# Attention's probability-value products as one 129-column matmul, with both heads of a tile in one PSUM bank

## The chip, the cores and the metric

The kernel runs on one core of one Trainium2 chip. The metric is device time in microseconds (us) of one execution of the whole program, as a median over runs. A profile of one further execution gives the durations of single instructions, the idle time of each engine and what ended it.

## What is computed

The reference is a two-layer encoder trunk on 2048 tokens of width 1024. Each layer normalises its input, projects it to 4096 columns, runs two kinds of heads side by side, gates both with a silu and projects back:

```
proj = rms_norm(x, gain) @ w_in            # aq ak av ag | rq rk rv rg
# A: 8 heads x 64, softmax over the own chunk of 64 and 8 chunks before it, with a relative bias
scores = q @ k.T * 64**-0.5 + bias ;  p = softmax(scores) ;  ya = p @ v
# B: 4 heads x 128, chunkwise retention with a state carried from chunk to chunk, and a norm per head
x = x + concat[ya * silu(ag), yr * silu(rg)] @ w_out
```

The change is in the last step of A: the product of the probabilities with the values, the division by the sum of the probabilities, and the gate.

## The kernel before

**Number format.** Products that need more than fp16 are split: a value is stored as an upper fp16 half and a lower fp16 half, and a product is the sum of three products of halves (upper-upper, upper-lower, lower-upper). The value tile `v` holds for each 128-token tile and head 129 columns: 64 upper halves, a column of ones, 64 lower halves. The column of ones makes the matmul deliver the sum of the probabilities as a 65th output column.

**Tiling.** For a layer `l`, `s` counts four slices of the heads (two attention heads and one retention head each), and `n` counts four blocks of 512 tokens. For each `(l, s, n)` there are the dense projections `dense_T` (L654, q and k and the retention's q and k, transposed) and `dense_V` (L785, values and gates), and later the `attention` (L823) of the same block, which runs beside the dense projections of the next block. A block has four tiles `a` of 128 tokens and two heads `hx`, so eight units. A unit looks back over `nb` of up to five 128-token blocks; there are 256 units and 1120 blocks in all.

**Order.** The order on TensorE, ScalarE, VectorE and GpSimd is written out by hand. `run` (L1219) takes the dense projections in rounds of eight 512-column matmuls. After each round it calls `tick`, which emits what is due on the deferred list (`later(k, fn)` puts `fn` k ticks ahead), and then one step of the attention. A unit takes three rounds. At its first round comes `flow`, which emits `pv` (L860) for the unit two before, and then `qk` (L830) for the new unit: the scores `S` on TensorE (L845, L846), bias and maximum on VectorE (L849, L851), the exponential and its upper half on ScalarE (L852, L854), the lower half on GpSimd (L855), and the transposing DMA `pT` (L857). The retention of a tile (L909) adds two groups of products `r1` and `r2` per six rounds, with VectorE and ScalarE work between them (L918, L903, L907: mask, upper half and rest of `dT`; L939: the state). Weight preparation for later slices is pushed into the same rounds; each weight section needs a sum over partitions, a one-column matmul `allsum` (L334).

**PSUM.** `psR` is a ring of four banks under the tag "small". In order of allocation it is used by `o` (the output of `pv`), `r1`, `r2` and the one-column sums. A new tile in a bank waits until the last reader of the tile before it is done. `psD` holds two banks for the dense projections; L697, L680 and L815 are the VectorE instructions that read them last.

**Around the change.** `pv` runs, for each block, three matmuls into 65 columns of a bank of its own (L865 to L867): upper probabilities with upper values and ones, upper probabilities with lower values, lower probabilities with upper values and ones. One tick later VectorE takes the reciprocal of the sum (L871), multiplies it by a constant (L872) and applies it and the gate (L877). After the second head of a tile the 128 columns are stored to DRAM by a DMA on SyncE's queue (L880).

Of the kernel before, what the change touches and what calls it, by code (L numbers as in the profile page):

```python
# [10 lines left out]
F32 = mybir.dt.float32  # L11
I32 = mybir.dt.int32
AF = mybir.ActivationFunctionType
ALU = mybir.AluOpType
# [4 lines left out]
P = 128  # L19
# [8 lines left out]
def hybrid_trunk(ctx: ExitStack, tc: tile.TileContext, x, pos, gain, gcol, w_in, w_out, rel, fgain,  # L28
# [8 lines left out]
    act, dve, pool, pe, sp = nc.scalar, nc.vector, nc.gpsimd, nc.tensor, nc.sync  # L37
# [5 lines left out]
    b2 = ctx.enter_context(tc.tile_pool(name="b2", bufs=2))  # L43
# [7 lines left out]
    psR = ctx.enter_context(tc.tile_pool(name="psR", bufs=4, space=PSUM))  # L51
# [16 lines left out]
    y_d = [dp.tile([P, D], F32, tag=f"y_d{t}", name=f"y_d{t}") for t in range(NT)]  # L68
# [554 lines left out]
    def in_turn(i):  # L623

        if not ring.get("free"):
            return
        tc.keep_in_program_order(i)


    def flow(k=0):  # L630

        if len(pipe) > k:
            pipe.pop(0)()
# [3 lines left out]
    def later(k, fn):  # L637
        deferred.append([k, fn])
# [184 lines left out]
    def attention(l, s, n, g, st, prev):  # L823
        units = []
        for a in range(4):
            for hx in range(2):
                units.append((a, hx))
        ya = {}

        def qk(a, hx):  # L830

            u = St()
            u.a, u.hx = a, hx
            u.nm = f"{l}_{s}_{n}_{a}_{hx}"
            u.nb = nb = min(5, 4 * n + a + 1)
            u.w = w = nb * P
            u.kts = [(st if t // 4 == n else prev, t % 4) for t in range(4 * n + a + 1 - nb, 4 * n + a + 1)]
            S = psS.tile([P, 1024], F32, tag="S", name=f"S{u.nm}")
            cs = slice(a * P, (a + 1) * P)
            cuts = sorted({0, nb} | {j for j in range(nb) if u.kts[j] == (st, 0) or j == 4})  # L840
            for j0, j1 in zip(cuts, cuts[1:]):
                q_, a_ = u.kts[j0]
                k_ = q_.k[:, hx, a_ * P:(a_ + j1 - j0) * P]
                o = S[:, j0 * P:j1 * P]
                pe.matmul(o, st.q[:, hx, 0, cs], k_, start=True, stop=False)  # L845
                pe.matmul(o, st.q[:, hx, 1, cs], k_, start=False, stop=True)  # L846
            v = b2.tile([P, 640], F32, tag="sc", name=f"sc{u.nm}")[:, 0:w]
            m = b2.tile([P, 1], F32, tag="mq", name=f"mq{u.nm}")
            dve.tensor_tensor_reduce(out=v, in0=S[:, 0:w], in1=g.bias[hx][:, 640 - w:640], scale=1.0, scalar=-3.0e38,  # L849
                                     op0=ALU.add, op1=ALU.max, accum_out=m)  # L850
            dve.tensor_scalar(m, m, g.nc[:, 0:1], LN_PSC, op0=ALU.mult, op1=ALU.add)  # L851
            act.activation(v, v, AF.Exp, bias=m[:, 0:1], scale=g.c[:, 0:1])  # L852
            pq = b2.tile([P, 1280], F16, tag="pq", name=f"pq{u.nm}")
            act.activation(pq[:, 0:w], v, AF.Copy)  # L854
            pool.tensor_tensor(pq[:, w:2 * w], v, pq[:, 0:w], op=ALU.subtract)  # L855
            u.p = b2.tile([P, 10, P], F16, tag="pT", name=f"pT{u.nm}")[:, 0:2 * nb, :]
            later(1, lambda: sp.dma_start_transpose(out=u.p, in_=pq[:, 0:2 * w]))  # L857
            return u

        def pv(u):  # L860
            t = 4 * n + u.a
            o = psR.tile([P, 512], F32, tag="small", name=f"o{u.nm}")
            for b, (q_, a_) in enumerate(u.kts):
                v_ = q_.v[:, a_, u.hx, :]
                pe.matmul(o[:, 0:65], u.p[:, b, :], v_[:, 0:65], start=(b == 0), stop=False)  # L865
                pe.matmul(o[:, 0:64], u.p[:, b, :], v_[:, 65:129], start=False, stop=False)  # L866
                pe.matmul(o[:, 0:65], u.p[:, u.nb + b, :], v_[:, 0:65], start=False, stop=(b == u.nb - 1))  # L867

            def out_():
                rl = b2.tile([P, 1], F32, tag="rl", name=f"rl{u.nm}")  # L870
                dve.reciprocal(rl, o[:, 64:65])  # L871
                dve.tensor_tensor(rl, rl, g.ka, op=ALU.mult)  # L872
                if u.hx == 0:
                    ya[u.a] = b2.tile([P, P], F32, tag="ya", name=f"ya{u.nm}")
                y = ya[u.a]
                vs = slice(u.hx * 64, u.hx * 64 + 64)
                dve.scalar_tensor_tensor(out=y[:, vs], in0=o[:, 0:64], scalar=rl[:, 0:1], in1=st.g[u.a][:, vs],  # L877
                                         op0=ALU.mult, op1=ALU.mult)
                if u.hx == 1:
                    later(1, lambda: in_turn(sp.dma_start(y_d[t][:, s * P:(s + 1) * P], y)))  # L880

            later(1, out_)

        ret = retention(l, s, n, g, st)
        rounds_ret = (5, 10, 10, 14, 14, 18, 18, 23) if (l, s, n) == (0, 0, 0) else [6 * a + b for a in range(4) for b in (0, 5)]
        for i, (a, hx) in enumerate(units):
            flow(1)
            u = qk(a, hx)
            for r in range(3 * i, 3 * i + 3):
                for _ in range(rounds_ret.count(r)):  # L890
                    next(ret, None)
                if r % 3 == 2:
                    pipe.append(lambda u=u: pv(u))
                yield
# [319 lines left out]
    def grp(l, s):  # L1214
        if (l, s) not in groups:
            groups[l, s] = Grp()
        return groups[l, s]
# [138 lines left out]
    for j in range(4):  # L1356
        o = VSEC[j] * 512
# [80 lines left out]
    for l in range(DEPTH):  # L1438
        gO = [Grp(), Grp()]
        go = Grp()  # L1440
        for s in range(NSW):
            g = grp(l, s)
            for n in range(NS):
                first = (l, s, n) == (0, 0, 0)
                if not first:
                    st = St()
                    states[l, s, n] = st
                    dT = dense_T(l, s, n, g, st)
                else:
                    st = st0  # L1450
# [129 lines left out]
```

## Time and profile before

| | |
|---|---|
| median of 3 runs | 2058.18 us (2057.85 to 2062.8) |
| span of the profiled execution | 2060.7 us |
| TensorE busy | 1999.4 us (97%), 14038 matmuls |
| VectorE busy | 1228.1 us (60%) |
| ScalarE busy | 1134.8 us (55%) |
| GpSimd busy | 688.1 us (33%) |
| mean granted TensorE clock | 0.995 |

The profiled execution's own time is its span of 2060.7 us, 2.5 us above the median of the runs. In the rows below, PE is TensorE's matmul side, PEld its weight loads, DVE VectorE, ACT ScalarE, POOL GpSimd and SP SyncE. [...] A group's row gives its busy time, the mean duration of one instruction in ns, and the engine's idle time just before it with what ended that.

### The profile page before, as it was taken

The page shows a single profiled execution, that of the slowest core. Times are in us where ns is not written, and L with a number is a line of the kernel's source. Part 1 is how long each engine was busy: PE and PEld are TensorE (multiplying, and loading weights), DVE is VectorE, ACT ScalarE, POOL GpSimd, SP SyncE. Part 2 cuts the span into 40 slices and gives each one's busy share as a digit, 9 for nine tenths or more (in the row PEclk, how much of TensorE's full clock was granted, in tenths as well). Part 3 has the DMA queues.
Part 4 walks back from the last instruction along what each step waited for, and adds up shares of the span by engine and source line. Part 5 has one row for each costly group of instructions (what it writes and reads, how often), then busy time and mean ns, then how long its engine had stood idle before and what let it go on. Part 6 is the DMA issues. An engine that isn't in the chain of part 4 may idle for free. (4 is left out here: it accounts for less than half of the span.)

```text
span 2060.7 us, 39339 instructions
## 1 busy us (share of the span) xinstructions
PE 1999.4 (97%) x14038; PEld 1052.9 (51%) x14038; DVE 1228.1 (60%) x3804; ACT 1134.8 (55%) x2526; POOL 688.1 (33%) x701
## 2 busy tenths in 40 slices
PE   6988999999999999999999999999999999999998
PEld 4444555555555555554444555555555555555544
DVE  6776666565556555666553556555655566557643
ACT  6556665556565645555444546655656565455432
POOL 0344343434334434430003443444333334333100
PEclk9999999999999999999999999999999999999999
DMA  8778664547584754899774546554746775658864
GB/s 227 169 161 178 155 148 109 112 114 164 117 185 113 165 128 101 174 209 263 219 185 113 124 104 156 116 126 103 158 117 150 148 155 124 129 115 187 224 203 139
DMA packets 645701, 313.64 MB, mean 152 GB/s; under 512 B 459232, under 2 KB 602080, under 8 KB 645504
## 3 DMA queue, kind: packets, MB, share of 16 engines
q1 hardware_dynamic: 645504, 311.12, 65.6%
q8 instruction: 110, 1.80, 0.4%
q14 instruction: 87, 0.71, 0.1%
HBM read 123.26 MB, written 41.98 MB: 80 GB/s over the span
## 5 line engine op out<-in xcount | busy, mean ns | idle before, releaser
L855 POOL TENSOR_TENSOR pq<-sc,pq 128x640 f16<-128x640 f32 (+4 forms) x256 | 319.4, 1248 | 860.5 <-ACT pq L854 443.8
L852 ACT ACTIVATE sc<-sc,mq,cT 128x640 f32<-128x640 f32 (+4 forms) x256 | 218.4, 853 | 615.6 <-DVE rl L871 309.7
L797 PE MATMUL dV<-whV,hTh 128*128 128x512 f16 x1024 | 353.9, 381 | 7.3 <-DVE gt L815 6.1
L797 PE MATMUL dV<-whV,hTl 128*128 128x512 f16 x1024 | 353.8, 381 | 0.0
L797 PE MATMUL dV<-wlV,hTh 128*128 128x512 f16 x1024 | 353.8, 381 | 0.0
L778 PE MATMUL dT<-hTh,whT 128*128 128x512 f16 x1008 | 346.6, 379 | 2.7 <-DVE kk L697 1.3
L778 PE MATMUL dT<-hTl,whT 128*128 128x512 f16 x1008 | 346.6, 379 | 0.0
L778 PE MATMUL dT<-hTh,wlT 128*128 128x512 f16 x1008 | 346.6, 379 | 0.0
L797 PEld LDWEIGHTS <-hTh 128*128 128x128 f16 x2048 | 197.0, 98 | 224.7 <-DVE gt L815 10.0
L778 PEld LDWEIGHTS <-whT 128*128 128x128 f16 x2016 | 192.1, 98 | 207.7 <-issue 1.6
L849 DVE CUSTOM_DVE_ANT_0 sc<-S,bias 128x640 f32<-128x640 f32 (+4 forms) x256 | 188.3, 735 | 88.8 <-PE S L846 87.4
L1172 PE MATMUL dO<-whO,yly 128*128 128x512 f16 x504 | 191.0, 379 | 1.7 <-DMA yly<-hTl 1.1
L1172 PE MATMUL dO<-whO,yhy 128*128 128x512 f16 x504 | 191.0, 379 | 1.0 <-DMA yhy<-hTh 1.0
L1172 PE MATMUL dO<-wlO,yhy 128*128 128x512 f16 x504 | 191.0, 379 | 0.0
L854 ACT ACTIVATE pq<-sc 128x640 f16<-128x640 f32 (+4 forms) x256 | 171.5, 670 | 8.1
L797 PEld LDWEIGHTS <-hTl 128*128 128x128 f16 x1024 | 99.4, 98 | 112.4 <-issue 3.9
L1172 PEld LDWEIGHTS <-yhy 128*128 128x128 f16 x1008 | 98.1, 98 | 113.7 <-DMA yhy<-hTh 1.5
L778 PEld LDWEIGHTS <-wlT 128*128 128x128 f16 x1008 | 97.2, 98 | 113.7 <-issue 6.0
L845 PE MATMUL S<-k,q 128*128 128x128 f16 (+3 forms) x592 | 142.4, 267 | 0.0
L865 PE MATMUL o<-v,pT 128*128 128x65 f16 x1120 | 129.8, 193 | 6.4 <-DMA pT<-pq 5.5
L866 PE MATMUL o<-v,pT 128*128 128x64 f16 x1120 | 130.1, 195 | 0.0
L846 PE MATMUL S<-k,q 128*128 128x128 f16 (+3 forms) x592 | 129.7, 267 | 0.0
(359 smaller groups left out, 3476.5 us busy)
## 6 DMA issues: line engine op xcount, KB each, us to landing
q<-qq SPq DMA_DIRECT2D x128, 128.0 KB, 2.4
yyy<-y_d SPq DMA_DIRECT2D x32, 512.0 KB, 4.5
stT<-in_w_in_dram SPq DMA_DIRECT2D x27, 512.0 KB, 4.8
stV<-in_w_in_dram SPq DMA_DIRECT2D x26, 512.0 KB, 4.6
k<-kk SPq DMA_DIRECT2D x128, 64.0 KB, 2.0
swp<-rot SPq DMA_DIRECT2D x64, 128.0 KB, 3.1
tabc<-tab SPq DMA_DIRECT2D x32, 256.0 KB, 3.0
tabs<-tab SPq DMA_DIRECT2D x32, 256.0 KB, 3.1
```

What stands on the lines that cost most here:

```text
L778: pe.matmul(ps, w_[:, j, kt, :], h_[:, kt, :], start=(m == 0), stop=(m == 23))
L797: pe.matmul(ps, h_[:, kt, a * P:(a + 1) * P], w_[:, kt, :], start=(m == 0), stop=(m == 23))
L845: pe.matmul(o, st.q[:, hx, 0, cs], k_, start=True, stop=False)
L846: pe.matmul(o, st.q[:, hx, 1, cs], k_, start=False, stop=True)
L849: dve.tensor_tensor_reduce(out=v, in0=S[:, 0:w], in1=g.bias[hx][:, 640 - w:640], scale=1.0, scalar=-3.0e38, op0=ALU.add, op1=ALU.max, accu ...
L852: act.activation(v, v, AF.Exp, bias=m[:, 0:1], scale=g.c[:, 0:1])
L854: act.activation(pq[:, 0:w], v, AF.Copy)
L855: pool.tensor_tensor(pq[:, w:2 * w], v, pq[:, 0:w], op=ALU.subtract)
L865: pe.matmul(o[:, 0:65], u.p[:, b, :], v_[:, 0:65], start=(b == 0), stop=False)
L866: pe.matmul(o[:, 0:64], u.p[:, b, :], v_[:, 65:129], start=False, stop=False)
L1172: pe.matmul(ps, h_[:, kt, :], w_[:, kt, :], start=(m == 0), stop=(m == 23))
```

## The change

The upper probabilities are multiplied with all 129 columns of `v` in one matmul, so that upper and lower values come out in separate columns of PSUM; the lower probabilities follow with 65 columns as before. Both heads of a tile write into one bank, 256 columns apart. Nothing is read after the first head. One tick after the second head's matmuls, ScalarE copies the lower values' products of both heads to SBUF and VectorE takes both reciprocals. One tick later VectorE adds the copy to the upper part (into free columns of the same bank), scales, and applies the gate for both heads in one instruction each. The DMA to DRAM moves by one tick with it. The tile `ya` now belongs to this step, and the ring `psR` is allocated from three times in six rounds and not four.

```diff
         def pv(u):
             t = 4 * n + u.a
-            o = psR.tile([P, 512], F32, tag="small", name=f"o{u.nm}")
+            if u.hx == 0:
+                ya[u.a] = psR.tile([P, 2, 256], F32, tag="small", name=f"o{u.nm}")
+            o = ya[u.a]
             for b, (q_, a_) in enumerate(u.kts):
                 v_ = q_.v[:, a_, u.hx, :]
-                pe.matmul(o[:, 0:65], u.p[:, b, :], v_[:, 0:65], start=(b == 0), stop=False)
-                pe.matmul(o[:, 0:64], u.p[:, b, :], v_[:, 65:129], start=False, stop=False)
-                pe.matmul(o[:, 0:65], u.p[:, u.nb + b, :], v_[:, 0:65], start=False, stop=(b == u.nb - 1))
+                pe.matmul(o[:, u.hx, 0:129], u.p[:, b, :], v_, start=(b == 0), stop=False)
+                pe.matmul(o[:, u.hx, 0:65], u.p[:, u.nb + b, :], v_[:, 0:65], start=False, stop=(b == u.nb - 1))
+            if u.hx == 0:
+                return
+            y = b2.tile([P, 2, 64], F32, tag="ya", name=f"ya{u.nm}")
+            rl = b2.tile([P, 2, 1], F32, tag="rl", name=f"rl{u.nm}")
+
+            def halves():
+                act.activation(y, o[:, :, 65:129], AF.Copy)
+                dve.reciprocal(rl, o[:, :, 64:65])
 
             def out_():
-                rl = b2.tile([P, 1], F32, tag="rl", name=f"rl{u.nm}")
-                dve.reciprocal(rl, o[:, 64:65])
-                dve.tensor_tensor(rl, rl, g.ka, op=ALU.mult)
-                if u.hx == 0:
-                    ya[u.a] = b2.tile([P, P], F32, tag="ya", name=f"ya{u.nm}")
-                y = ya[u.a]
-                vs = slice(u.hx * 64, u.hx * 64 + 64)
-                dve.scalar_tensor_tensor(out=y[:, vs], in0=o[:, 0:64], scalar=rl[:, 0:1], in1=st.g[u.a][:, vs],
-                                         op0=ALU.mult, op1=ALU.mult)
-                if u.hx == 1:
-                    later(1, lambda: in_turn(sp.dma_start(y_d[t][:, s * P:(s + 1) * P], y)))
-
-            later(1, out_)
+                w = o[:, :, 192:256]
+                dve.tensor_tensor(w, y, o[:, :, 0:64], op=ALU.add)
+                dve.scalar_tensor_tensor(out=w, in0=w, scalar=g.ka[:, 0:1], in1=rl.to_broadcast([P, 2, 64]), op0=ALU.mult,
+                                         op1=ALU.mult)
+                dve.tensor_tensor(y, w, st.g[u.a][:, 0:P].rearrange("p (h d) -> p h d", h=2), op=ALU.mult)
+                yf = y.rearrange("p h d -> p (h d)")
+                later(1, lambda: in_turn(sp.dma_start(y_d[t][:, s * P:(s + 1) * P], yf)))
+
+            later(1, halves)
+            later(2, out_)
```

## The prediction

> **What bounds the kernel now.** I read the page's first part, then the table of stretches. Columns of a stretch: its length, then the busy time of PE, PEld, DVE, ACT and POOL.
>
> ```profile
> span 2060.7 us, 39339 instructions
> PE 1999.4 (97%) x14038; PEld 1052.9 (51%) x14038; DVE 1228.1 (60%) x3804; ACT 1134.8 (55%) x2526; POOL 688.1 (33%) x701
> ```
>
> ```profile
> 80.00:360.00 280.00, 261.50 (x1839) 136.35 (x1838) 179.99 (x588) 170.47 (x384) 104.78 (x106) 0.98 0.68 148
> 1100.00:1360.00 260.00, 260.00 (x1875) 137.75 (x1874) 147.37 (x521) 147.53 (x351) 98.53 (x98) 1.00 0.53 120
> ```
>
> TensorE is the bound: in the middle of layer 1 it is busy for all of 260 us, and only in the first attention blocks does it lose something (18.5 of 280 us). A TensorE saving counts in full, and a new wait costs only if TensorE ends up waiting. So I next read who waits for whom (total us, times, longest).
>
> ```profile
> DVE sc L849 <- PE S L846: 87.4, 89, 2.4
> ACT sc L852 <- DVE rl L871: 309.7, 106, 3.9
> ACT sc L852 <- DVE mq L851: 250.9, 124, 3.5
> PEld L899 <- DVE dT L907: 12.8, 11, 2.6
> PEld L797 <- DVE gt L815: 10.0, 5, 3.8
> ```
>
> ```profile
> PE r L899 <- DVE dT L907: 6.8, 9, 1.6
> PE dV L797 <- DVE gt L815: 6.1, 4, 3.3
> PE msV L334 <- DVE ya L877: 3.4, 3, 1.5
> ```
>
> These rows carry the forecast. Of 256 score scans (L849) VectorE waits for TensorE before 89 only; at the other 167 the scores lay ready and VectorE came late. ScalarE's exponential waits on VectorE in 106 + 124 = 230 of 256 units. So VectorE runs behind TensorE in most units, although it is busy 60% of the time: its loss is in the order of its queue. Its lateness reaches TensorE in 11 + 5 + 9 + 4 + 3 = 32 places, 39.1 us together, 1.2 us each.
>
> **Part 1: the matmuls.** The timeline of TensorE over one unit (start, duration):
>
> ```profile
> 1204.74 0.19 PE L865 MATMUL o<-v,pT 128*128 128x65 f16 x1
> ...
> 1205.18 0.19 PE L867 MATMUL o<-v,pT 128*128 128x65 f16 x1
> 1205.21 0.38 PE L845 MATMUL S<-k,q 128*128 128x512 f16 x1
> ...
> 1205.75 0.33 PE L899 MATMUL r<-rot,rot 128*128 128x128 f16 x3
> 1205.92 0.38 PE L778 MATMUL dT<-hTh,wlT 128*128 128x512 f16 x1
> ```
>
> ```profile
> L865 PE MATMUL o<-v,pT 128*128 128x65 f16 x1120 | 129.8, 193 | 6.4 <-DMA pT<-pq 5.5 <-DVE ya L877 0.8
> L866 PEld LDWEIGHTS <-pT 128*128 128x128 f16 x1120 | 104.9, 97 | 28.6 <-issue 0.6
> ```
>
> The 15 products of a unit start within 1204.74 to 1205.21, 0.47 us: 31 ns each, 94 ns for the three of a block. Three 128-column products take 0.17 us (1205.75 to 1205.92): 57 ns each, and 129 columns the same. After the change a block costs 57 + 31 = 88 ns, so 6 ns less, times 1120 blocks: **7 us saved**. Bounds: 0 if the short product behind a long one costs 37 ns, 11 us if they cost 55 and 29. The columns that pass through the array stay the same (65 + 64 + 65 against 129 + 65 per block); only the spacing of one short product goes.
>
> The removed products' weight loads take 97 ns each, but follow each other at 31 ns beside the products, so nothing more comes from them. [...]
>
> **Part 2: the new wait.** VectorE and ScalarE around a second head's output now:
>
> ```profile
> 1212.30 0.82 DVE L849 CUSTOM_DVE_ANT_0 sc<-S,bias 128x640 f32<-128x640 f32 x1 [0.42 <-PE S L846]
> ...
> 1213.30 0.16 DVE L871 RECIPROCAL rl<-o 128x1 f32<-128x1 f32 x1
> 1213.49 0.16 DVE L872 TENSOR_TENSOR rl<-rl,kaV 128x1 f32<-128x1 f32 x1
> 1213.69 0.28 DVE L877 SCALAR_TENSOR_TENSOR ya<-o,rl,gt 128x64 f32<-128x64 f32 x1
> 1216.38 0.69 DVE L697 SCALAR_TENSOR_TENSOR kk<-dT,kk 128x512 f16<-128x512 f32 x1 [2.41 <-ACT kk L694]
> 1216.99 0.28 DVE L939 SCALAR_TENSOR_TENSOR state<-r,state 128x128 f32<-128x128 f32 x1
> 1219.00 0.83 DVE L849 CUSTOM_DVE_ANT_0 sc<-S,bias 128x640 f32<-128x640 f32 x1 [1.72 <-PE S L846]
> ```
>
> ```profile
> 1213.48 0.92 ACT L852 ACTIVATE sc<-sc,mq,cT 128x640 f32<-128x640 f32 x1 [3.14 <-DVE rl L871]
> 1214.43 0.74 ACT L854 ACTIVATE pq<-sc 128x640 f16<-128x640 f32 x1
> ...
> 1215.76 0.60 ACT L694 ACTIVATE kk<-dT 128x512 f16<-128x512 f32 x1 [0.39 <-PE dT L778]
> ```
>
> In the changed program's built order the reciprocal of every one of the 128 tiles waits for ScalarE's copy of the lower half, not for TensorE; the copy stands behind the exponential and the copy of the unit just started:
>
> ```
> VectorE: L849, L851 | Reciprocal rl<-o 128x2 [waits Activation] | L880 | L881 | L883 | L697 or L811 to L815 | state | L849
> ScalarE: L852 exp, L854 copy | L875 ya<-o 128x128 | evacuation of the dense product
> ```
>
> [...]
>
> Prices of the new steps from the nearest shapes:
>
> ```profile
> L903 ACT ACTIVATE dT<-r 128x128 f16<-128x128 f32 x128 | 33.5, 261 | 0.4 <-DVE r L918 0.4
> L918 DVE TENSOR_TENSOR r<-r,msk 128x128 f32<-128x128 f32 x128 | 37.1, 290 | 0.0
> L956 DVE SCALAR_TENSOR_TENSOR yr<-r,rss,gt 128x128 f32<-128x128 f32 x128 | 44.4, 347 | 23.5 <-POOL rss L952 22.5
> L805 ACT ACTIVATE v<-dV 128x128 f16<-128x128 f32 x128 | 33.5, 261 | 11.8 <-PE dV L797 11.4
> L806 ACT ACTIVATE gt<-dV,ughV 128x256 f32<-128x256 f32 x128 | 59.2, 462 | 0.5 <-DVE ya L877 0.4
> L807 ACT ACTIVATE rv<-dV,urvV 128x128 f16<-128x128 f32 x128 | 46.5, 363 | 0.0
> ```
>
> ScalarE's copy: 0.26 us. VectorE: 0.16 + 0.29 + 0.35 + 0.29 = 1.09 us and three hand-overs of 0.03 us (1213.30 + 0.16 to 1213.49): 1.2 us, where two heads now take about 2 x 0.67 us (1213.30 to 1213.97). So work falls slightly; the waiting is what counts. In this tile the reciprocal would wait from 1213.30 until the copy behind L854 is out at 1215.4, and the chain ends at 1216.6, not 1213.97: 2.6 us later.
>
> Behind it in VectorE's queue are the rest of the dense product (L697, or L811 to L815), the state, the next score scan, and `dT`'s rest (L907); ScalarE's next exponential waits for that scan, TensorE for L907 and, through psD, for L697 and L815. Much of the 2.6 us is covered, as L697 waits for ScalarE today (2.41 us). What cover remains is ScalarE's evacuation after the copy. In a `dense_T` round that is 0.60 us, so L697 comes later by 0.26 + (1.2 - 0.6) = 0.86 us; in a `dense_V` round it is 0.26 + 0.46 + 0.36 = 1.08 us, so 0.26 + (1.2 - 1.08) = 0.38 us. Mean **d = 0.62 us** per tile; lower end 0.2 us (this tile, where ScalarE had 0.39 us to spare: 1216.6 against 1216.38), upper end the whole 2.6 us where nothing behind waits for ScalarE.
>
> Where VectorE waits for the scores (1.72 us before the last scan above), d costs nothing. Where TensorE already waits for VectorE, it costs d in full: 32 x 0.62 = 20 us. Near misses come on top: 32 waits spread over a mean of 1.2 us suggest 32 x 0.62 / 1.2 = 17 places within reach, at half of d: 5 us. **25 us lost**; with the lower end 6 + 1 = 7 us, and with 0.86 us in every tile 28 + 10 = 38 us.
>
> **Part 3: the ring.** With three tiles per six rounds in a ring of four banks, a bank comes round after eight rounds, not six, and `o` is held from the first head's product until the gate of both. Its own products are late enough for that, but the one-column sums fall in between. There are 55 of them:
>
> ```profile
> L334 PEld LDWEIGHTS <-ones x55: 97/98/105, 0.9 to 1685.3; 128*128 128x128 bf16 x55
> ```
>
> In the built order 11 wait for L883, where 9 wait for L877 now, of which 3 cost 3.4 us. With the bank free 2.6 us later I let all 11 wait those 1.1 us: 12 - 3.4, about **8 us lost**; bounds 0 and 11 x 2.6 = 28 us.
>
> **Moved at no cost.** The store's DMA is issued one tick later, in SyncE's order in front of the next unit's transposes; the transposes of the unit under way stand before it. If that cover goes, `pT` comes late: TensorE's wait for it at L865 is 5.5 us in all today.
>
> **Sum.** 2060.7 - 7 + 25 + 8 = 2086.7 us as a span; the median of the runs lies 2.5 us below the span: **2084 us**, slower by 1.3%. A measurement of this kernel can tell about 0.3% (6 us) from no change.
>
> **Rivals.**
> - *The waits stay hidden, TensorE's saving is left.* The place is the middle of the layers, where TensorE has no idle time and VectorE's wait for ScalarE is there anyhow. For it: 1100 to 1360 us. Against it: 167 late scans. 2058 - 7 = 2051 us. It decides if VectorE's chain still ends before L697 and L815 could start. Chance 0.15.
> - *Both about cancel:* d at its lower end and no ring waits, -7 + 7: 2058 us. Chance 0.10.
> - *VectorE and ScalarE become the bound.* If the 2.6 us fall on VectorE uncovered in the 32 places and the 17 become 32 x 2.6 / 1.2 = 69 at half, that is 83 + 90 us less what the queue catches up; already half of it gives 2058 + 87 - 7 + 8 = 2146 us. Against it: VectorE is free 40% of the time. Chance 0.09.
> - *Weight loads are paid in full.* If each removed load costs its 97 ns, 1120 x 97 = 109 us go: 1949 us. Against it stands the 31 ns spacing. Chance 0.02. [...]
>
> **The numbers.** The forecast as worked out has 0.64. Its own bounds are 2058 - 11 + 7 = 2054 and 2058 + 38 + 28 - 7 = 2117 us. The range of 2050 to 2118 takes in the second rival and the centre of the first; left out are the third, the fourth and some of the first, about 0.18. Slower by over 0.3%: 0.64 + 0.09 = 0.73; within 0.3%: 0.10; faster: 0.15 + 0.02 = 0.17.
>
> **What would show it.** TensorE's unit of ten products should take 5 x 88 = 0.44 us for 0.47, PE's busy time fall by some 7 us and its idle time rise by 30 to 40 us. The waits should name VectorE's reciprocal waiting for ScalarE's L875, about 2 us in most of the 128 tiles, and TensorE waiting longer for `dT` (L913) and, at L334, for L883. I am wrong if TensorE's waits for VectorE stay near 39 us in total: then the cover held. If they grow, but at the accesses of `pT` or `S`, the place was wrong.

## The result, and the profile after

The changed kernel takes 2088.6 us (median of 4 runs, 2087.37 to 2089.82) against 2059.3 us of the kernel before beside it: a ratio of 1.0137, 95% interval 1.0123 to 1.0152, so 28 us slower by the ratio and 29 us by the two medians. The forecast was 2084 us.

The page of the kernel after, first part:

```profile
span 2085.6 us, 37004 instructions
PE 2005.0 (96%) x12918; PEld 1049.8 (50%) x12918; DVE 1205.8 (58%) x3548; ACT 1155.2 (55%) x2654; POOL 680.6 (33%) x701
```

There are 1120 matmuls fewer, and yet TensorE is busy for 5.6 us longer (1999.4 before) and idle for 80.6 us instead of 61.3. Its unit of ten products, on the timeline of the kernel after (start, duration):

```profile
1230.67 0.22 PE L867 MATMUL o<-v,pT 128*128 128x129 f16 x1
1230.73 0.20 PE L868 MATMUL o<-v,pT 128*128 128x65 f16 x1
...
1231.08 0.19 PE L868 MATMUL o<-v,pT 128*128 128x65 f16 x1
1231.11 0.38 PE L845 MATMUL S<-k,q 128*128 128x512 f16 x1
```

From 1230.67 to 1231.11 it is 0.44 us for the ten, where the fifteen took 0.47. Each is shown with 0.19 to 0.22 us and starts 0.03 to 0.06 us ahead of the next, so the unit is counted from start to start and not by the shown durations. So the matmuls did what the diff says; the loss is elsewhere. The waits of the kernel after (total us, times, longest):

```profile
DVE rl L876 <- ACT ya L875: 250.8, 120, 4.7
DVE sc L849 <- PE S L846: 40.4, 50, 2.0
ACT sc L852 <- DVE mq L851: 558.2, 232, 5.1
PEld L905 <- DVE dT L913: 30.8, 30, 3.5
```

and those of TensorE's two sides alone:

```profile
PE r L905 <- DVE dT L913: 24.0, 25, 3.7
PE msV L334 <- DVE ya L883: 4.8, 3, 2.6
PE msT L334 <- DVE mbT L327: 4.8, 5, 1.7
PE msO L334 <- DVE ya L883: 2.1, 2, 1.1
PE dV L797 <- DVE gt L815: 3.9, 5, 1.6
PEld L334 <- DVE ya L883: 8.7, 6, 2.8
PEld L797 <- DVE gt L815: 6.7, 8, 2.1
```

The first row is the new wait: the reciprocal stands for 250.8 us in 120 of the 128 tiles behind ScalarE's copy, 2.1 us each. The second shows how far VectorE fell behind: it came to the score scan before TensorE had the scores 89 times before the change and 50 times now. The price is paid where TensorE waits for `dT`.

The rows of PEld and of PE must not be added up, though the prediction adds them: they show the same stalls from two sides. One stall of the kernel after, on the timelines of the two sides (start, duration, idle time before it):

```profile
195.04 0.10 PEld L905 LDWEIGHTS <-dT 128*128 128x128 f16 x1 [1.27 <-DVE dT L913]
195.05 0.23 PE L905 MATMUL r<-rv,dT 128*128 128x128 f16 x1 [1.10 <-DVE dT L913]
```

In the kernel before, all 9 waits of PE for `dT` and all 4 for `gt` lie within a wait of PEld; in the kernel after it is 24 of 25 for `dT`, and 5 of 5 each for `gt` at L797 and for `ya` at L334. PE's side is the idle time of the matmuls: 24.0 us for `dT`, where it was 6.8; at the one-column sums (L334) 4.8 + 2.1 = 6.9 us for 3.4; at the dense values (L797) it fell, 3.9 for 6.1. Together that is 34.8 us in place of 16.3, a rise of 18.5 us, near the 19.3 us by which TensorE's idle time rose in all. A wait that the kernel before does not have, 4.8 us in 5 places for `mbT` (L327, VectorE's weight preparation), comes up as well, and other waits fell. The prediction and the expectations count both sides together; on that scale `dT` is 30.8 + 24.0 = 54.8 us in place of 19.6.

VectorE around one tile's gate, on the timeline of the kernel after:

```profile
1232.73 0.21 DVE L851 TENSOR_SCALAR mq<-mq,ncT 128x1 f32<-128x1 f32 x1
1235.12 0.17 DVE L876 RECIPROCAL rl<-o 128x2 f32<-128x2 f32 x1 [2.18 <-ACT ya L875]
1235.32 0.30 DVE L880 TENSOR_TENSOR o<-ya,o 128x128 f32<-128x128 f32 x1
1235.65 0.36 DVE L881 SCALAR_TENSOR_TENSOR o<-o,kaV,rl 128x128 f32<-128x128 f32 x1
1236.05 0.29 DVE L883 TENSOR_TENSOR ya<-o,gt 128x128 f32<-128x128 f32 x1
1236.26 0.68 DVE L697 SCALAR_TENSOR_TENSOR kk<-dT,kk 128x512 f16<-128x512 f32 x1
1238.53 0.82 DVE L849 CUSTOM_DVE_ANT_0 sc<-S,bias 128x640 f32<-128x640 f32 x1 [1.39 <-PE S L846]
```

VectorE has nothing to do for 2.18 us, although reciprocal, gate and L697 are queued. The four instructions of the gate end at 1236.34, 1.22 us after the reciprocal's start. Here the scan behind them still has 1.39 us to wait, so at the scan this tile costs nothing; one without that slack passes its lateness on.

The stretches of the kernel after (columns as in the prediction; behind POOL's the granted clock, the DMA share and GB/s):

```profile
80.00:360.00 280.00, 254.08 (x1615) 131.27 (x1614) 170.30 (x518) 166.28 (x386) 101.54 (x104) 0.96 0.66 144
1100.00:1360.00 260.00, 258.46 (x1673) 134.78 (x1672) 135.59 (x439) 143.20 (x352) 96.67 (x101) 1.00 0.54 122
```

Between 80 and 360 us TensorE is idle 25.9 us for 18.5 before, 7.4 of the 19.3 us, and its clock is 0.96 for 0.98. In the middle of layer 1, where it had no idle time, it now has 1.5 of 260 us.

### The profile page after: what moved, and what is told of

Its sections match the earlier page's. It is cut to its first block, busy times and chain, and to the rows that moved or that the text cites. A ratio compares the mean times of both kernels' runs of the same rounds, so it can differ in the third digit from the quotient of the medians.

```text
span 2085.6 us, 37004 instructions
## 1 busy us (share of the span) xinstructions
PE 2005.0 (96%) x12918; PEld 1049.8 (50%) x12918; DVE 1205.8 (58%) x3548; ACT 1155.2 (55%) x2654; POOL 680.6 (33%) x701
## 5 line engine op out<-in xcount | busy, mean ns | idle before, releaser
L855 POOL TENSOR_TENSOR pq<-sc,pq 128x640 f16<-128x640 f32 (+4 forms) x256 | 319.5, 1248 | 898.6 <-ACT pq L854 467.8
L797 PE MATMUL dV<-whV,hTh 128*128 128x512 f16 x1024 | 353.1, 381 | 4.0 <-DVE gt L815 3.9
L797 PE MATMUL dV<-whV,hTl 128*128 128x512 f16 x1024 | 352.9, 380 | 0.0
L797 PE MATMUL dV<-wlV,hTh 128*128 128x512 f16 x1024 | 352.6, 380 | 0.0
L797 PEld LDWEIGHTS <-hTh 128*128 128x128 f16 x2048 | 196.5, 98 | 219.0 <-DVE gt L815 6.7
L854 ACT ACTIVATE pq<-sc 128x640 f16<-128x640 f32 (+4 forms) x256 | 171.5, 670 | 8.1
L876 DVE RECIPROCAL rl<-o 128x2 f32<-128x2 f32 x128 | 21.7, 170 | 250.8 <-ACT ya L875 250.8
L797 PEld LDWEIGHTS <-hTl 128*128 128x128 f16 x1024 | 99.2, 98 | 115.8 <-issue 7.7
L867 PE MATMUL o<-v,pT 128*128 128x129 f16 x1120 | 133.4, 222 | 3.6 <-DMA pT<-pq 2.8
```

The source lines that it names most:

```text
L797: pe.matmul(ps, h_[:, kt, a * P:(a + 1) * P], w_[:, kt, :], start=(m == 0), stop=(m == 23))
L867: pe.matmul(o[:, u.hx, 0:129], u.p[:, b, :], v_, start=(b == 0), stop=False)
L876: dve.reciprocal(rl, o[:, :, 64:65])
```

## The experiments

Each is compared with the kernel before on the same chip; that took 2060.3 us beside `mm_alone`, `wait_alone`, `early_copy` and `dve_copy`, 2061.1 us beside `early_out1`, `ring_alone` and `wait_nomul`, and 2061.6 us beside `after_out1`.

**1. The matmuls alone (`mm_alone`).**

```diff
-                pe.matmul(o[:, 0:65], u.p[:, b, :], v_[:, 0:65], start=(b == 0), stop=False)
-                pe.matmul(o[:, 0:64], u.p[:, b, :], v_[:, 65:129], start=False, stop=False)
+                pe.matmul(o[:, 0:129], u.p[:, b, :], v_, start=(b == 0), stop=False)
```

> The kernel before with only its matmuls changed: upper probabilities times all 129 columns in one matmul, each head still in a bank of its own, and VectorE's three instructions per head as they were. The lower values' product (columns 65 to 128) is computed and not read, so the output lacks that term. Theory A (the loss of the change comes from VectorE's reciprocal waiting for ScalarE's copy): TensorE's saving is left alone, 4 to 7 us under the kernel before, about 2054 us against 2059. Theory B (the loss comes from the ring of banks): the same, since the ring is as before. If it is not faster, the matmul term of the sum was wrong. The share of waits stays as before (retention's products for dT near 20 us).

Measured: 2054.2 us, ratio 0.9970 (0.9959 to 0.9982). The page of this kernel:

```profile
span 2050.8 us, 37100 instructions
PE 1991.7 (97%) x12918; PEld 1047.6 (51%) x12918; DVE 1232.4 (60%) x3804; ACT 1134.5 (55%) x2526; POOL 688.4 (34%) x701
```

TensorE's busy time is 7.7 us below that of the kernel before and the median 6.1 us below. So one matmul of 129 columns for two short ones is worth what the spacing on the timeline said, and not a weight load each.

**2. The wait alone (`wait_alone`).** The kernel before, with a ScalarE copy from and into the second head's bank put ahead of that head's reciprocal:

```diff
             def out_():
                 rl = b2.tile([P, 1], F32, tag="rl", name=f"rl{u.nm}")
+                if u.hx == 1:
+                    act.activation(o[:, 256:320], o[:, 0:64], AF.Copy)
                 dve.reciprocal(rl, o[:, 64:65])
```

> The kernel before with the wait alone: its matmuls, its banks and its VectorE instructions stay, but at every second head ScalarE first copies 64 columns of the output bank to free columns of the same bank, so that the reciprocal behind it has to wait for ScalarE (128 times). Theory A: slower by 20 to 33 us, 2080 to 2092 us, with TensorE's waits for dT near 50 us, as in the changed kernel. Theory B: the ring is as before, so no more than a few us, 2059 to 2064. Theory C (ScalarE's added work of 128 copies is what costs, wherever it stands): slower by 15 to 25 us as well; the next kernel tells A and C apart.

Measured: 2101.0 us, ratio 1.0194 (1.0178 to 1.0210), more than any of the expectations had. Its waits, and its multiplication by the constant in the view of groups by shape:

```profile
DVE rl L873 <- ACT o L871: 244.5, 120, 4.6
```

```profile
L874 DVE TENSOR_TENSOR rl<-rl,kaV 128x1 f32<-128x1 f32 x256 | 122.3, 478 | 8.8
```

The wait is that of the changed kernel (244.5 us in 120 tiles for 250.8). But the multiplication, an operation on 128x1 elements that the changed kernel doesn't have, takes 478 ns on average; in the kernel before it is

```profile
L872 DVE TENSOR_TENSOR rl<-rl,kaV 128x1 f32<-128x1 f32 x256 | 55.8, 218 | 8.9
```

218 ns. That made this kernel a poor stand-in, and led to experiment 3.

**3. The wait without that multiplication (`wait_nomul`).**

```diff
-                dve.tensor_tensor(rl, rl, g.ka, op=ALU.mult)
+                if u.hx == 0:
+                    dve.tensor_tensor(rl, rl, g.ka, op=ALU.mult)
```

> The kernel before with the wait alone, as measured at 2101 us, but without the multiplication of the second head's 128x1 reciprocal by its constant (left out, so the output of the second heads lacks that factor). With the wait that 128x1 multiplication took 478 ns in the mean where it takes 218 ns in the kernel before, since it then falls on GpSimd's subtraction (L855). Theory A with this as a second price: the time falls by 6 to 18 us, to 2083 to 2095 us, and the wait of the reciprocal stays near 245 us. If the lengthening has no part in it: 2098 to 2101 us.

Measured: 2078.1 us, ratio 1.0078 (1.0062 to 1.0093): 23 us less than `wait_alone`, and 17 us more than the kernel before, with the old matmuls, the old banks and the gate at its old tick. The wait of the reciprocal is again 244.5 us in 120 tiles. TensorE's matmul side at the retention's products:

```profile
PE r L902 <- DVE dT L910: 14.3, 18, 2.4
```

14.3 us for 6.8 in the kernel before, 7.5 us more. TensorE's idle time in all rose by 10.9 us (2076.1 - 2003.9 = 72.2 for 61.3) and its busy time by 4.5 us. The wait alone, without the other parts of the change, makes the kernel slower. Its price is not read off exactly: this kernel has 128 multiplications less than the kernel before, so its 17 us may be too little, and the 41 us of `wait_alone` hold the lengthened multiplication too.

**4. The wait taken out of the changed kernel (`early_copy`).** ScalarE's copy is emitted directly behind the second head's matmuls, ahead of the next exponential in ScalarE's order, and not a tick later:

```diff
+            act.activation(y, o[:, :, 65:129], AF.Copy)
+
             def halves():
-                act.activation(y, o[:, :, 65:129], AF.Copy)
                 dve.reciprocal(rl, o[:, :, 64:65])
```

> The changed kernel with ScalarE's copy emitted at once behind the second head's matmuls, so that it stands in ScalarE's queue before the exponential of the unit just started and not behind its exponential and copy. Matmuls, shared bank, ring, ScalarE's and VectorE's work are all those of the changed kernel. Theory A: VectorE's wait for the copy is gone (250.8 us to under 20 us), the time falls by 26 to 34 us to 2054 to 2062 us, and the waits for dT fall from 54.8 to near 20 us. Theory B: the bank is held as long as in the changed kernel, so it stays at 2075 to 2088 us. Theory C: ScalarE does the same work, so 2080 to 2089 us.

Measured: 2064.1 us, ratio 1.0014 (1.0006 to 1.0023): 24.6 us less than the changed kernel, and 2 us above the upper end of what I had expected for it. Its groups by shape:

```profile
L874 ACT ACTIVATE ya<-o 128x128 f32<-128x128 f32 x128 | 34.9, 272 | 63.9 <-PE o L868 63.9
L877 DVE RECIPROCAL rl<-o 128x2 f32<-128x2 f32 x128 | 20.5, 160 | 0.0
```

The idle time before the reciprocal is 0.0 us. The copy itself now waits 63.9 us for the matmuls. VectorE on this kernel's timeline:

```profile
1228.44 0.21 DVE L851 TENSOR_SCALAR mq<-mq,ncT 128x1 f32<-128x1 f32 x1
1228.57 0.16 DVE L877 RECIPROCAL rl<-o 128x2 f32<-128x2 f32 x1
1228.76 0.29 DVE L881 TENSOR_TENSOR o<-ya,o 128x128 f32<-128x128 f32 x1
```

Between L851 and the reciprocal, where the changed kernel had 2.18 us, there is no gap. And TensorE's matmul side at the retention's products:

```profile
PE r L906 <- DVE dT L914: 12.7, 13, 2.5
```

12.7 us for 24.0 (both sides together 29.1 us for 54.8; near 20 us was expected). TensorE's idle time in all fell by 13.0 us, from 80.6 to 67.6, and its busy time by 9.9 us, to 1995.1. Theories B and C fall with this run: the bank is held as long and ScalarE does the same work, and 24.6 us of the loss are gone. The loss is not longer VectorE instructions either, as VectorE is busy for 1205.1 us here and 1205.8 us in the changed kernel.

**5. The copy on VectorE (`dve_copy`).** The same step at its late place, as `dve.tensor_copy`, so that the reciprocal has no copy of another engine to wait for.

```diff
-                act.activation(y, o[:, :, 65:129], AF.Copy)
+                dve.tensor_copy(y, o[:, :, 65:129])
```

> The changed kernel with the copy of the lower values' products on VectorE in place of ScalarE, at the same place of the order; all else as in the changed kernel. Theory A: no engine waits for another over the shared bank, 2054 to 2064 us, although VectorE gets 128 x 0.25 us = 32 us more to do. Theory B: the bank is held as long, 2075 to 2088 us. Theory C: ScalarE's work is gone, 2054 to 2064 us as with A.

Measured: 2061.9 us, ratio 1.0010 (1.0001 to 1.0019). Its groups by shape:

```profile
L875 DVE COPY ya<-o 128x128 f32<-128x128 f32 x128 | 35.9, 281 | 0.0
L876 DVE RECIPROCAL rl<-o 128x2 f32<-128x2 f32 x128 | 20.3, 158 | 0.0
```

VectorE does 128 x 0.28 = 36 us of copies that it does not have in the changed kernel (its busy time in all is 1231.1 us for 1205.8), and the kernel is 26.7 us faster. So it is not VectorE's work that the change made too long, but its place in the queue behind ScalarE.

**6. Shared bank and ring without the copy (`ring_alone`).** The matmuls of `mm_alone`, both heads in one bank, three tiles of the ring per six rounds; the old VectorE steps of both heads follow in a row one tick after the second head.

```diff
-            o = psR.tile([P, 512], F32, tag="small", name=f"o{u.nm}")
+            if u.hx == 0:
+                ob[u.a] = psR.tile([P, 2, 256], F32, tag="small", name=f"o{u.nm}")
+            o = ob[u.a][:, u.hx, :]
...
+            if u.hx == 0:
+                first_out[u.a] = out_
+                return
+            later(1, first_out[u.a])
             later(1, out_)
```

> The kernel with only the matmuls changed, plus the shared bank: both heads of a tile in one bank, 256 columns apart, three allocations of the ring per six rounds; VectorE's six small instructions for both heads follow one tick after the second head. No copy on ScalarE; the lower values' product is not read, so the output lacks that term. Theory A2: the ring itself costs 0 to 3 us, 2054 to 2057 us. Theory B2: it costs the 10 us that the early copy left, 2062 to 2065 us.

Measured: 2061.0 us, ratio 0.9998 (0.9989 to 1.0007), 7 us more than `mm_alone`. It lies between the two ranges and doesn't decide between the theories: it carries six VectorE instructions in a row where the changed kernel has four, and TensorE's wait for `dT` grew with it (PE's side 11.2 us, `mm_alone` 8.8 us). At the one-column sums the wait for `ya` is 3.0 us, 2 times, no more than the 3.4 us before. So the shared bank, with the gate one tick after the second head, need not cost anything there.

**7. The gate one tick earlier, with the early copy (`early_out1`).** `early_copy`, and

```diff
-            later(2, out_)
+            later(1, out_)
```

> The kernel with the early copy, and the gate (sum, scaling, gate of both heads) one tick earlier, in the same tick as the reciprocal: the bank is read out one tick sooner and the store is issued one tick sooner. The early copy alone left 10 us over the kernel with only the matmuls changed. Theory A2 (what is left comes from the bank, and the VectorE work behind it, being a tick late): it falls by 6 to 10 us to 2054 to 2058 us, faster than the kernel before by 2 to 6 us, and the waits for dT and at L334 go back to those of the kernel before (19.6 and 3.4 us). Theory B2 (what is left comes from the ring of four banks being used three times per six rounds, or from the copy on ScalarE): it stays at 2061 to 2065 us.

Measured: 2055.8 us, ratio 0.9974 (0.9963 to 0.9986): 8.3 us less than `early_copy`, and the one version with the change's banks and fused gate that beats the kernel before. TensorE's matmul side at the retention's products and at the one-column sums:

```profile
PE r L906 <- DVE dT L914: 8.8, 11, 1.6
PE msV L334 <- DVE ya L884: 4.0, 3, 1.8
```

In `early_copy` they are 12.7 us and 4.3 + 2.1 = 6.4 us, in the kernel before 6.8 and 3.4. TensorE's idle time in all fell by 7.6 us, from 67.6 to 60.0. The store moves with the gate, so the step is the price of both; TensorE's wait for `pT`, which a late store could delay, is 5.7 us for 6.8. The median stays 1.6 us above `mm_alone`, which is less than these runs can tell apart.

**8. The gate one tick earlier, with the late copy (`after_out1`).** The same edit of one line, made in the changed kernel.

> The changed kernel with the gate one tick earlier, in the same tick as the copy and the reciprocal, and the copy still behind the exponential in ScalarE's queue. With the early copy this step of one tick was worth 8 us. If the tick is a price of its own beside the wait: 2078 to 2082 us. If the wait for ScalarE hides it (VectorE stands at the reciprocal until about then anyhow, and nothing stands between the two ticks in its queue): 2085 to 2089 us.

Measured: 2100.3 us, ratio 1.0190 (1.0172 to 1.0209). Both theories missed: it is 12 us slower than the changed kernel, not 8 us faster or equal. TensorE's matmul side (total us, times, longest):

```profile
PE r L905 <- DVE dT L913: 17.4, 21, 2.2
PE r L905 <- DVE m2T L336: 8.2, 8, 1.3
PE msT L334 <- DVE mbT L327: 7.9, 7, 1.4
```

The reciprocal waits as before (250.6 us in 120 tiles), and TensorE waits less for `dT` (17.4 us for 24.0). But 8 stalls of 8.2 us come up at the retention's products that the changed kernel doesn't have, behind the weight preparation (L336), which VectorE has in its queue between the two ticks; at the weight loads, 7 of these 8 stalls show as waits for the gate (L883). The wait for `mbT` at the one-column sums grew by 3.1 us. My reading is that with the gate at the earlier tick these steps stand behind reciprocal and gate, and so behind ScalarE; with the gate at the later tick they overtook it. The order of the queue that this rests on is in the emission; that it explains all 12 us is argued and not shown.

## Why the prediction was right, and where it wasn't

The medians give the change in four steps: matmuls -6.1 us (`mm_alone` against before), the reciprocal behind ScalarE +24.6 us (changed kernel against `early_copy`), the gate at the second tick +8.3 us (`early_copy` against `early_out1`), and +1.6 us for the rest (`early_out1` against `mm_alone`). The prediction's terms were -7, +25 and +8. The runs were taken in several sittings, in which the kernel before stood between 2059.3 and 2061.6 us, so a step is known to about 2 us.

- **Part 1** held in mechanism and size: 0.44 us for the unit of ten, 6.1 us in the median of `mm_alone`.
- **Part 2** held in mechanism: the reciprocal waits 2.1 us in 120 of 128 tiles, and taking that wait out in two ways (`early_copy`, `dve_copy`) gives 25 and 27 us back. Its sum was wrong. The 32 places are waits of PEld and of PE added up, and these are the same stalls: counted once they are 11 + 5 + 3 = 19 places, with 16.3 us of idle matmuls. By the prediction's own rule 19 places give 12 us, and 19 x 0.62 / 1.2 = 10 near misses give 3 us, so 15 us and not 25; the forecast would have been 2074 us. What made up for it is that more places came within reach: counted at the weight loads, 30 + 8 + 6 = 44 stalls after the change, 25 more than before, where the rule gives 10 more. They are not spread alike either: PE's waits for `dT` rose by 17.2 us, and those at L797 fell by 2.2. That 32 x 0.62 + 5 came out at the measured 24.6 us is luck.
- **Part 3** has the size of another cause. I let 11 one-column sums wait; the 11 waits for `ya` that the view of L334 has are 6 stalls, 5 of them seen from both sides, and the idle time there rose by 3.5 us (6.9 for 3.4), not by 8. With the same ring and the gate alone moved (`early_out1`) it is 4.0 us, so less than 1 us is left for the ring; what it paid for was the late gate. The prediction gave the gate's second tick no price of its own, and the store one tick later it put under "Moved at no cost"; the tick is 8.3 us with the early copy, of which PE's waits have 3.9 us at `dT` and 2.4 us at L334. With the late copy the sign turns round (experiment 8), so these four steps add up along this path only and are no prices of their own.
- **The signpost on busy and idle time failed.** I expected TensorE's busy time to fall by 7 us and its idle time to rise by 30 to 40. Busy time rose by 5.6 us, 13.3 us above `mm_alone`; idle time rose by 19.3. The step that failed is the reading of a wait's whole price as idle time. Of the 34.8 us between the spans of `mm_alone` and of the changed kernel, 21.5 us are idle time and 13.3 us busy time. A stall is shown shorter as idle time of the matmuls than at the weight load: the one above has 1.10 us for 1.27, and its first 0.17 us stand under busy time. The clock behind the waits was lower too (below): its mean is 0.993 for 0.996 in `mm_alone`, and 0.003 x 2086 = 6 us of the 13.3 is an estimate from that. The rest I put to that first part of the stalls, without a run that shows it in all.
- **The rivals.** The one in which the waits stay hidden falls with `wait_nomul`, which is 17 us slower by the wait alone. The one in which VectorE becomes the bound falls with `dve_copy`: more VectorE work, less time. The one in which saving and losses about cancel falls with the result. Weight loads paid in full falls with `mm_alone`: 6 us, not 109.

## What to carry to other kernels

When two engines read one bank, look at where the other engine's read stands in its own queue before pricing the read: the copy of 0.27 us cost 25 us because it was emitted behind an exponential; emitted ahead of it, and with the gate at the earlier tick, it left no more than 2 us over the matmuls alone. The wait on VectorE, which was 58% busy, was paid by what stood behind it in VectorE's order (TensorE's waits for `dT`: 24.0 us for 6.8), so name that work and its consumer, and move the step in front of the long one before looking for a cheaper instruction. Count a stall once: of the 25 waits of the matmuls for `dT`, 24 lay within a wait of the weight loads. And move one thing at a time: the same shift by one tick gave 8 us with the early copy and took 12 us with the late one.

## What the runs showed of the hardware

**A 128x1 instruction that took up to 1.2 us.** In `wait_alone`, the multiplication behind the reciprocal, on the timelines of VectorE and of GpSimd:

```profile
1218.53 0.17 DVE L873 RECIPROCAL rl<-o 128x1 f32<-128x1 f32 x1 [2.58 <-ACT o L871]
1218.73 0.43 DVE L874 TENSOR_TENSOR rl<-rl,kaV 128x1 f32<-128x1 f32 x1
```

```profile
1217.75 1.40 POOL L855 TENSOR_TENSOR pq<-sc,pq 128x640 f16<-128x640 f32 x1 [3.40 <-ACT pq L854]
```

The multiplication ends at 1219.16, GpSimd's L855 at 1219.15. Over the run the 256 multiplications take 158 to 1227 ns; 147 of them start while GpSimd is busy, and take 714 ns on average; the other 109 take 159 ns. Of the 147, 136 end within 0.06 us of the GpSimd instruction that was under way. In the kernel before, 45 of the 256 start while GpSimd is busy, and take 493 ns on average; the other 211 take 159 ns, and 44 of the 45 end within 0.06 us of the GpSimd instruction under way. In the tile shown, ScalarE's L854 releases GpSimd's L855 at 1217.75 and ScalarE's copy releases the reciprocal at 1218.53, so the wait for ScalarE moved this step into GpSimd's work. Why the two end together no run shows. `wait_nomul`, which leaves the 128 multiplications of the second heads out, is 23 us faster than `wait_alone`; how much of that is the lengthening and how much the multiplications themselves was not measured apart.

**A clock of 0.51 behind two waits of 1.1 us.** Stretches of the kernel after (behind the busy times of the five engines stand the granted clock, the DMA share and GB/s):

```profile
188.00:195.40 7.40, 5.25 (x41) 2.68 (x38) 4.81 (x14) 4.86 (x12) 1.95 (x2) 1.00 0.70 171
195.40:202.30 6.90, 5.59 (x26) 2.79 (x26) 2.77 (x12) 3.23 (x8) 1.40 (x1) 0.51 1.03 219
202.30:209.00 6.70, 6.70 (x44) 3.40 (x42) 3.26 (x11) 3.82 (x9) 1.95 (x2) 1.00 0.27 64
```

and TensorE's timeline at the first border:

```profile
193.49 0.29 PE L905 MATMUL r<-rv,dT 128*128 128x128 f16 x2 [1.05 <-ACT dT L909]
195.05 0.23 PE L905 MATMUL r<-rv,dT 128*128 128x128 f16 x1 [1.10 <-DVE dT L913]
196.76 0.61 PE L778 MATMUL dT<-hTh,whT 128*128 128x512 f16 x1 [1.31 <-DMA hTh<-xa]
```

Two waits of 1.05 and 1.10 us, 1.6 us apart, and the clock is 0.51 for the next 6.9 us; a dense product of 0.38 us is shown with 0.61. Without the 1.31 us of its own wait TensorE is busy for 5.59 us of this stretch; at a clock of 1.00 that work could have been done in up to 5.59 x 0.49 = 2.7 us less, an estimate from the two numbers. If the two waits lowered the clock, which no run without them tests, they cost up to that much more than their own 2.2 us. No pause in the 7.4 us ahead of the fall was longer than 1.10 us (the 1.31 us came behind it). What lowered the clock is not shown.
